# Turning keys, values and mLSTM outputs by VectorE squares and transfers instead of TensorE transposes, in a two-layer recurrent decoder step

## The chip, the cores and the metric

The kernel runs on one core of a Trainium2 chip. The metric is the device time of one execution in microseconds (us), the median over runs. The engines are named as in the profile: PE (TensorE matmuls), PEld (TensorE weight loads), DVE (VectorE), ACT (ScalarE), POOL (GpSimd), SP (the queue that issues the transfers).

## What is computed

One step of a two-layer decoder with 1024 prompt tokens and 8 sample rows that share the weights. Everything is float32. Each layer normalizes its input, projects it with one large matrix, mixes it over time in recurrent heads, multiplies by a gate and projects back:

```python
def _even_mixer(h, ...):            # layer 0
    proj = h @ w_in
    u_a, beta_pre, a_pre, q_b, k_b, v_b, if_pre, o_pre, z = _split(proj, EVEN_SPLIT)
    q_a, k_a, v_a = _split(silu(causal_conv(u_a)), ...)      # 8 gated-delta heads, key 128, value 128
    o_a, new_gdn = _gated_delta(q_a, k_a, v_a, beta, g_a, s_gdn)
    h_b, new_mc, new_mn, new_mm = _mlstm(q_b, k_b, v_b, ...)  # 8 mLSTM heads, key 64, value 128
    h_b = sigmoid(o_pre) * _rms(h_b, mlstm_norm_w)
    y = concat([_rms(o_a), h_b]) * silu(z)
    return y @ w_out, ...
def _odd_mixer(h, ...):             # layer 1
    ...                             # 4 gated linear attention heads, 4 retention heads, key 128, value 256
```

The recurrences are computed in chunks. For the gated delta rule a chunk solves a unit lower triangular system `(A + 1) U = rhs`, with `A` built from the products of keys.

## The kernel before

**Layout.** Activations lie with channels on the 128 partitions and the 1024 + 8 tokens (`W` = 1032) along the free dimension. Chunks have `L` = 128 tokens, so there are `NC` = 8 chunks. A projection of 128 output channels is 72 matmuls: three token blocks of 344, eight slices of the inner dimension, and three products, because each float32 factor is split into a high and a low part in the fast type fp32r (`halves` makes `whi` on ACT and `wlo` on DVE).

**Where a turn is needed.** The chunk recurrences need keys and values with tokens on the partitions. Before, the even layer turns them on PE: `transpose4` runs four 128x128 transposes into a PSUM bank, and DVE or ACT carries the result off while scaling it. `gdn_mix` does so for `k2` and `v2` of each of the 8 gated-delta heads (16 transposes a head, into the slots `kd` and `vs`), `mlstm_pair_mix` for the keys `mk` of each of 4 pairs of heads (8 transposes, into `kwe`), `mlstm_mix` for the values (into `va`), and `mlstm_out` turns the output `hn` of each mLSTM head back (8 transposes). In the odd layer `v_tokens` turns values with `by_token`, which is 16 DVE transposes of 32x256 for one [128, 1024] tile.

**The triangular inverse.** `inverse` takes the diagonal blocks of the 128x128 matrices `N`: it inverts 8x8 blocks on DVE (blocks fetched through DRAM by `nd` and `yd`, then seven steps of two small DVE operations), doubles them to 16 and to 32 in two passes on PE (each pass two groups of 32 products of 32x32), and then to 64 and 128.

**Order.** The program is recorded first, and every instruction gets a rank. A planner (`Recorder.order`) runs a list scheduler over the recorded operations forward and backward, with a table of assumed durations (`_cost`, `_pe_cost`, the latencies of transfers), and writes out each engine's instructions in the order that it found. The engines then run their rows strictly in that order, and a row waits for its semaphores. All transfers go through SP's one queue. The order thus interleaves the projections of coming heads with the recurrences of earlier ones. `self.nc.after` adds a dependency to all operations recorded while it is set.

**Layer boundary.** `out_proj` of the even layer loads the rows of the mixed output `y` back from DRAM (`yd`) into staging slots, splits them (`split`, ACT for the high part, DVE or POOL for the low part, into the slots `s_h` and others) and multiplies. Rows 0 to 7 are the gated-delta heads, rows 8 to 15 the mLSTM heads; the last, row 15, comes straight from `mlstm_out` of head 7. `odd_setup` loads the odd layer's constants (`lmask`, `rdm`, `rin`, `rend`, `cosT`, `sinT`), some of them into the `arena` that the even layer's small tiles used.

All instructions are issued by the recorder's helper, so all have one line in the profile (L451 before); groups are told apart by the names of their tiles.

Of the kernel before, what the change touches and what calls it, by code (L numbers as in the profile page):

```python
# [17 lines left out]
T = 1024  # L18
# [21 lines left out]
def host_constants():  # L40
# [24 lines left out]
    code = np.zeros((32, 32), f)  # L65
    for i in range(2):
        code[lm[:, 1 - i, :].T > 0] = 1.0 + i
    c["icode"] = np.tile(code, (4, 1))
    c["i8"] = np.tile(np.eye(8, dtype=f).reshape(1, 64), (128, 1))
# [39 lines left out]
def _cost(queue, method, out, args, kw):  # L109
# [4 lines left out]
    if queue == "vector":  # L114
# [4 lines left out]
        if method == "transpose":  # L119
            return 436.0, False  # L120
# [18 lines left out]
def _pe_cost(method, out, args, kw):  # L139
# [6 lines left out]
    if kw.get("tile_position") is not None and cols <= 32:  # L146
        return (max(1.87 * n / 4, 15.0) if rows > 32 else 15.0), (rows, cols)
# [319 lines left out]
class Step:  # L467
# [733 lines left out]
    def gdn_mix(self, h, k2, q2, v2, z2):  # L1201
# [4 lines left out]
        kd = self.slot("kd", [128, NC, L], name="kd")  # L1206
        ksq = self.slot("N", [128, NC, L], name="ksq")
        for g in range(2):
            p = self.transpose4(k2, g)
            p3 = p.rearrange("p (c d) -> p c d", d=L)  # L1210
            self.act(ksq[:, 4 * g:4 * g + 4, :], p3, AF.Square)
            V.tensor_tensor(kd[:, 4 * g:4 * g + 4, :], p3,
                            self.g_kdec[:, 4 * g:4 * g + 4, h].unsqueeze(2).to_broadcast([128, 4, L]), op=ALU.mult)
# [7 lines left out]
        vs = self.slot("vs", [128, NC, L], name="vs")  # L1221
        for g in range(2):
            p = self.transpose4(v2, g)
            V.tensor_tensor(vs[:, 4 * g:4 * g + 4, :], p.rearrange("p (c d) -> p c d", d=L),
                            kk[:, 2, 4 * g:4 * g + 4].unsqueeze(2).to_broadcast([128, 4, L]), op=ALU.mult)
# [31 lines left out]
        for g in range(2):  # L1257
            po = self.ps(i=g)
            for i in range(4):
# [4 lines left out]
                w = vs[:, c, :]  # L1264
                if S is not None:
                    self.mm(pc[:, 0, :], k2[:, s], S)
                    w = self.small([128, L], "w", bufs=1)
                    V.scalar_tensor_tensor(w, pc[:, 0, :], self.g_ngam[:, c, h:h + 1], vs[:, c, :], op0=ALU.mult,
# [5 lines left out]
                self.mm(pc[:, 2, :], kd[:, c, :], U)  # L1274
# [18 lines left out]
    def inverse(self, N):  # L1293
# [6 lines left out]
        by8 = lambda x: x[:, 0:256].rearrange("m (r t) -> m r t", t=32)[:, :, 0:8]  # L1300
        blocks = [slice(32 * j, 32 * j + 32) for j in range(4)]
        for j, b in enumerate(blocks):
            dma(by32(nd, j), N[b, :, b])
        n8, y8, t8 = (self.const([128, 8, 8], x) for x in ("n8", "y8", "t8"))
        dma(n8, by8(nd))
        G.tensor_copy(y8, self.i8)
        for s in range(7):
            n = 7 - s
            V.tensor_tensor(t8[:, 0:s + 1, 0:n], y8[:, 0:s + 1, s:s + 1].to_broadcast([128, s + 1, n]),
                            n8[:, s:s + 1, s + 1:8].to_broadcast([128, s + 1, n]), op=ALU.mult)  # L1310
            V.tensor_tensor(y8[:, 0:s + 1, s + 1:8], y8[:, 0:s + 1, s + 1:8], t8[:, 0:s + 1, 0:n], op=ALU.subtract)
        dma(by8(yd), y8)

        t = self.slot("EM", name="inv")
        D, At, qt, Dt = (t[:, 256 * i:256 * i + 256].rearrange("p (c t) -> p c t", c=NC) for i in range(4))
# [3 lines left out]
        for i in range(1, 3):  # L1319
            p = self.ps(None, [128, NC, 32])  # L1320
            for c in range(NC):
                for j, b in enumerate(blocks):
                    self.mm(p[b, c, :], N[b, c, b], Dt[b, c, :], tile_position=(32 * j, 32 * j))
# [623 lines left out]
    def out_proj(self, src, l, mod):  # L1947
# [107 lines left out]
        for k in late:  # L2055
            split(k)
# [197 lines left out]
```

## Time and profile before

| | |
|---|---|
| runs | 2294.88, 2287.2, 2292.83 us, median 2292.83 |
| profiled execution | 2289.05 us, span in the profile 2287.0 us |
| PE busy | 2221.4 us, 97% of the span |
| PEld busy | 2070.0 us |
| DVE busy | 1382.8 us (60%) |
| ACT, POOL busy | 747.7 us, 527.7 us |
| mean granted PE clock | 0.987 |
| transfers | 235.20 MB, mean 103 GB/s |

"Busy" is the time in which at least one instruction of an engine runs, as a share of the span. The duration of one matmul in the profile covers its way through the array, and the next starts before it ends; the pace is read from the distance of the starts. Because PE is busy nearly all the time, the idle time of other engines costs nothing unless PE waits for them.

### The profile page before, as it was taken

The page shows a single profiled execution, that of the slowest core. Times are in us where ns is not written, and L with a number is a line of the kernel's source. Part 1 is how long each engine was busy: PE and PEld are TensorE (multiplying, and loading weights), DVE is VectorE, ACT ScalarE, POOL GpSimd, SP SyncE. Part 2 cuts the span into 40 slices and gives each one's busy share as a digit, 9 for nine tenths or more (in the row PEclk, how much of TensorE's full clock was granted, in tenths as well). Part 3 has the DMA queues.
Part 4 walks back from the last instruction along what each step waited for, and adds up shares of the span by engine and source line. Part 5 has one row for each costly group of instructions (what it writes and reads, how often), then busy time and mean ns, then how long its engine had stood idle before and what let it go on. Part 6 is the DMA issues. An engine that isn't in the chain of part 4 may idle for free.

```text
span 2287.0 us, 44726 instructions
## 1 busy us (share of the span) xinstructions
PE 2221.4 (97%) x18844; PEld 2070.0 (91%) x18844; DVE 1382.8 (60%) x2700; ACT 747.7 (33%) x1374; POOL 527.7 (23%) x385
## 2 busy tenths in 40 slices
PE   6999999999999999999989999999999999998998
PEld 5777788899999999899989999999999999997997
DVE  6774646565564646556453355876976876977332
ACT  4422323232233233232331134234225324334322
POOL 3121112111123012211330031422422422433100
PEclk8999999999999999999999999999999999998999
DMA  9362544422143212432362221233142143246222
GB/s 260 124 165 60 152 133 121 129 77 72 40 118 105 69 52 86 108 95 72 114 216 84 75 76 38 56 122 107 43 136 94 50 133 95 56 149 209 74 58 91
DMA packets 285455, 235.20 MB, mean 103 GB/s; under 512 B 47819, under 2 KB 257733, under 8 KB 285246
## 3 DMA queue, kind: packets, MB, share of 16 engines
q1 hardware_dynamic: 285254, 232.35, 34.6%
q8 instruction: 147, 2.41, 0.4%
q14 instruction: 54, 0.44, 0.1%
HBM read 185.59 MB, written 46.91 MB: 102 GB/s over the span
## 4 chain that ended last, share of the span: by engine, by line
PE 88%; DMA 4%; DVE 4%; issue 1%; ACT 1%; POOL 1%; SPq 1%; POOLq 0%; DVEq 0%; ACTq 0%
PE pj L451 68%; PE A L451 14%; PE B L451 6%; DMA wf<-in_ev_w_in 1%; SPq L451 1%; DMA s_aT<-rd 0%; DVE s_h L451 0%; DMA s_h<-in_x_prompt 0%; DVE arena L451 0%; DVE s_N L451 0%; DMA s_pt<-yd 0%; DVE s_pt L451 0%; DMA ed<-s_Y 0%; DMA s_mp<-gd 0%; DVE s_mp L451 0%
## 5 line engine op out<-in xcount | busy, mean ns | idle before, releaser
L451 PE MATMUL pj<-s_h,whi 128*128 128x344 f32 (+1 forms) x6024 | 1498.6, 327 | 10.8 <-ACT s_h L451 5.4
L451 PEld LDWEIGHTS pj<-s_h,whi 128*128 128x128 f32 (+1 forms) x6024 | 1042.7, 189 | 44.8 <-issue 25.3
L451 PE MATMUL pj<-s_h,wlo 128*128 128x344 f32 (+1 forms) x3024 | 982.2, 325 | 1.5 <-DVE wlo L451 0.9
L451 PEld LDWEIGHTS pj<-s_h,wlo 128*128 128x128 f32 (+1 forms) x3024 | 569.8, 189 | 16.1 <-issue 10.6
L451 DVE TENSOR_TENSOR wlo<-wf,whi 128x1024 fp32r<-128x1024 f32 (+1 forms) x144 | 192.9, 1340 | 291.2 <-ACT whi L451 272.3
L451 ACT ACTIVATE whi<-wf 128x1024 fp32r<-128x1024 f32 (+2 forms) x146 | 152.1, 1043 | 374.9 <-PE pj L451 330.3
L451 ACT ACTIVATE s_pt<-pj 128x344 f32<-128x344 f32 (+1 forms) x170 | 77.0, 453 | 288.3 <-PE pj L451 282.8
L451 POOL TENSOR_TENSOR arena<-arena,base 128x8 f32<-128x8 f32 (+5 forms) x38 | 64.4, 1697 | 377.8 <-DVE arena L451 377.1
L451 POOL TENSOR_TENSOR s_tmp<-s_EM 128x512 f32<-128x512 f32 (+1 forms) x60 | 88.5, 1493 | 156.2 <-PE A L451 69.1
L451 DVE SCALAR_TENSOR_TENSOR s_pt<-s_u,base,s_pt 128x1024 f32<-128x1024 f32 x72 | 96.5, 1341 | 0.3
L451 ACT ACTIVATE s_u<-pj 128x344 f32<-128x344 f32 x93 | 41.9, 453 | 142.4 <-PE pj L451 80.2
L451 DVE SCALAR_TENSOR_TENSOR arena<-arena,A 128x128 f32<-128x128 f32 (+1 forms) x84 | 32.8, 391 | 84.5 <-PE A L451 83.9
L451 DVE STREAM_TRANSPOSE s_kd<-s_u 32x256 f32<-32x256 f32 x128 | 55.8, 436 | 16.6 <-ACT s_u L451 13.5
L451 POOL TENSOR_TENSOR s_tmp<-s_tmp,arena 128x1024 f32<-128x1024 f32 (+2 forms) x26 | 43.4, 1676 | 88.6 <-PE A L451 62.2
L451 POOL TENSOR_TENSOR s_kd<-s_kd,s_vs 128x1032 f32<-128x1032 f32 x8 | 21.5, 2688 | 167.6 <-ACT s_vs L451 152.2
L451 DVE SCALAR_TENSOR_TENSOR s_zz<-s_pt,pj 128x344 f32<-128x344 f32 x96 | 48.4, 507 | 18.7 <-ACT s_pt L451 17.9
L451 DVE STREAM_TRANSPOSE s_vs<-s_v 32x256 f32<-32x256 f32 x128 | 55.8, 436 | 1.9
L451 ACT ACTIVATE arena<-A,arena 128x128 f32<-128x128 f32 x64 | 23.5, 368 | 100.8 <-PE A L451 100.5
L451 ACT ACTIVATE s_tmp<-s_tmp 128x1024 f32<-128x1024 f32 (+1 forms) x44 | 46.1, 1054 | 28.7 <-POOL s_tmp L451 24.0
L451 DVE SCALAR_TENSOR_TENSOR arena<-arena,B 64x130 f32<-64x130 f32 (+1 forms) x84 | 31.2, 371 | 38.6 <-PE B L451 37.2
L451 ACT ACT_TABLE_LOAD x41 | 52.6, 1283 | 5.2 <-DMA s_h<-in_x_prompt 4.5
L451 POOL MEMSET s_u<- 128x3 f32 x24 | 2.4, 101 | 208.5 <-DVE s_pt L451 208.5
(643 smaller groups left out, 3597.7 us busy)
## 6 DMA issues: line engine op xcount, KB each, us to landing
wf<-in_ev_w_in SPq DMA_DIRECT2D x64, 512.0 KB
wf<-in_od_w_in SPq DMA_DIRECT2D x48, 512.0 KB
wf<-in_ada_w SPq DMA_DIRECT2D x32, 512.0 KB
s_pt<-yd SPq DMA_DIRECT2D x24, 516.0 KB
s_tmp<-sd SPq DMA_DIRECT2D x24, 512.0 KB
yd<-s_qg SPq DMA_DIRECT2D x15, 516.0 KB
wf<-in_ev_w_out SPq DMA_DIRECT2D x14, 512.0 KB
wf<-in_od_w_out SPq DMA_DIRECT2D x14, 512.0 KB
```

Source lines behind the costliest of these rows:

```text
L451: op.fn(*[self.placed(x) for x in op.args], **{k: self.placed(x) for k, x in op.kw.items()})
```

## The change

A new method `squares` turns a [128, 1024] tile without PE. One DVE instruction transposes all squares of 32x32 within their place and writes each with a step of 8 elements; a transfer of 512 KB puts the tile in a DRAM scratch (`td`, four of them), and four transfers of 128 KB read it back, one for each band of 32 partitions, so that the squares land in their turned place. The chunk number is then the fastest index: the slice of one chunk, `[:, c]`, has a step of 8 elements, 32 bytes, between its columns.

`squares` replaces the PE transposes of `k2` and `v2` (`gdn_mix`), `mk` (`mlstm_pair_mix`) and `hn` (`mlstm_out`); the mLSTM values stay on PE. The scaling by chunk that rode on the copy out of PSUM is now a separate DVE multiplication in place. In the odd layer `v_tokens` uses `squares` too, instead of 32 small DVE transposes a head; the turned keys there stay with `by_token`.

Other parts: `inverse` starts with 16x16 blocks on DVE (15 steps of two operations on 64 partitions) and so has one PE pass instead of two; in the odd layer every second `wlo` is made on POOL; the odd layer's constants wait for the last split of the even layer (`split_at`); the planner's assumed durations of DVE transposes and small matmuls are altered.

```diff
@@ planner @@
         if method == "transpose":
-            return 436.0, False
+            return 100 + 1.31 * n, False
...
     if kw.get("tile_position") is not None and cols <= 32:
-        return (max(1.87 * n / 4, 15.0) if rows > 32 else 15.0), (rows, cols)
+        return (max(0.8 * n, 20.0) if rows > 32 else 18.0), (rows, cols)
@@ halves @@
-        self.nc.vector.tensor_tensor(lo, w[:, 0:n], hi, op=ALU.subtract)
+        (self.nc.gpsimd if self.layer == "odd" and self.turn("half", 2) else self.nc.vector).tensor_tensor(lo, w[:, 0:n], hi, op=ALU.subtract)
@@ gdn_mix @@
-        kd = self.slot("kd", [128, NC, L], name="kd")
+        kd = self.squares(self.slot("kd", name="kd"), k2)
         ksq = self.slot("N", [128, NC, L], name="ksq")
-        for g in range(2):
-            p = self.transpose4(k2, g)
-            p3 = p.rearrange("p (c d) -> p c d", d=L)
-            self.act(ksq[:, 4 * g:4 * g + 4, :], p3, AF.Square)
-            V.tensor_tensor(kd[:, 4 * g:4 * g + 4, :], p3, ...)
+        self.act(ksq, kd, AF.Square)
+        by_c = lambda y, t: V.tensor_tensor(y, y, t.unsqueeze(1).to_broadcast([128, y.shape[1], NC]), op=ALU.mult)
+        by_c(kd.rearrange("p c d -> p d c"), self.g_kdec[:, :, h])
...
-        vs = self.slot("vs", [128, NC, L], name="vs")
-        for g in range(2):
-            p = self.transpose4(v2, g)
-            V.tensor_tensor(vs[:, 4 * g:4 * g + 4, :], ...)
+        vs = self.squares(self.slot("vs", name="vs"), v2)
+        by_c(vs.rearrange("p c d -> p d c"), kk[:, 2, :])
...
-                self.mm(pc[:, 2, :], kd[:, c, :], U)
+                self.mm(pc[:, 2, :], kd[:, c], U)
@@ inverse @@
-        for s in range(7):
+        for s in range(15):
...
-        for i in range(1, 3):
-            p = self.ps(None, [128, NC, 32])
...
+        p = self.ps(None, [128, NC, 32])
...
@@ mlstm_pair_mix @@
+        kwe = self.squares(self.slot("kwe", name="kwe"), self.mk)
+        for x in range(2):
+            t = kwe.rearrange("p c d -> p d c")[:, 64 * x:64 * x + 64, :]
+            V.tensor_tensor(t, t, self.g_we[:, :, 2 * p + x].unsqueeze(1).to_broadcast([128, 64, NC]), op=ALU.mult)
@@ mlstm_out @@
-        for g in range(2):
-            t = self.ps()
-            for i in range(4):
-                self.tr(t[:, 128 * i:128 * i + 128], hn[:, 4 * g + i, :])
-            s = slice(512 * g, 512 * g + 512)
-            V.scalar_tensor_tensor(y[:, s], t, self.nw[:, 1:2], oz[:, s], op0=ALU.mult, op1=ALU.mult)
+        t = self.squares(self.slot("va", name="ht"), hn.rearrange("p c d -> p (c d)"))
+        y3 = y[:, 0:T].rearrange("p (c t) -> p c t", c=NC)
+        V.scalar_tensor_tensor(y3, t, self.nw[:, 1:2], y3, op0=ALU.mult, op1=ALU.mult)
@@ odd_setup @@
+        self.nc.after = (self.split_at,)
         self.lmask = self.c_load("lmask", [128, 6, 32])
...
@@ new, and v_tokens @@
+    def squares(self, y, x):
+        dma = self.nc.sync.dma_start
+        y = y[:, 0:T]
+        self.nc.vector.transpose(y.rearrange("p (b j c) -> p b c j", b=4, c=NC),
+                                 x[:, 0:T].rearrange("p (c b i) -> p b c i", b=4, c=NC))
+        d = self.td[self.turn("td", 4)]
+        dma(d, y)
+        for b in range(4):
+            dma(y[32 * b:32 * b + 32].rearrange("i (a x) -> i a x", a=4),
+                d.rearrange("(a i) (b x) -> b i a x", a=4, b=4)[b])
+        return y.rearrange("p (d c) -> p c d", c=NC)
     def v_tokens(self, v):
-            self.by_token(t, v[i])
+        return [self.squares(self.slot(tag, name="vt"), v[i]) for i, tag in enumerate(("kd", "vs"))]
```

The change gives the planner other work and other durations, so all engines' rows stand in another order. Three places matter below.

PE, at the sixth gated-delta head. Before, the keys (`s_k`) are transposed between two projection matmuls (`pj`):

```order
L451 MATMUL pj_111<-s_h_604,whi_107 128x344
L451 MATMUL A_114<-base,s_k_63 128x128 x4
L451 MATMUL A_115<-base,s_k_63 128x128 x4
L451 MATMUL pj_111<-s_h_618,whi_107 128x344
L451 MATMUL pj_111<-s_h_604,wlo_109 128x344
```

After, no transposes stand there; the products of the keys with themselves (`A<-s_k`) and with the queries (`A<-s_q,s_k`) follow the projection directly:

```order
L448 MATMUL pj_111<-s_h_707,whi_107 128x344
L448 MATMUL pj_111<-s_h_727,whi_107 128x344
L448 MATMUL pj_111<-s_h_707,wlo_109 128x344
L448 MATMUL A_114<-s_k_63 128x128
L448 MATMUL A_115<-s_k_63 128x128
L448 MATMUL A_113<-s_k_63 128x128
L448 MATMUL pj_112<-s_h_447,whi_106 128x344
L448 MATMUL pj_112<-s_h_458,whi_106 128x344
L448 MATMUL pj_112<-s_h_447,wlo_108 128x344
L448 MATMUL A_114<-s_q_64,s_k_63 128x128
```

What moved: the two rows of transposes are gone from PE, and nothing of the turn is left there.

SP, the same head's key turn after the change (`td` is the scratch in DRAM, `s_kd` the turned tile):

```order
L448 DMA td_129<-s_kd_66 128x1024
L448 DMA out_s_conv<-arena 8x128
L448 DMA wf_105<-in_ev_w_in 128x8x128
L448 DMA s_kd_66<-td_129 32x4x256 x4
L448 DMA td_130<-s_vs_67 128x1024
```

What moved: five new transfers stand in the queue, the four that read back behind the one that writes, with one small transfer and one weight load between them, and the values' turn behind them.

SP, at the layer boundary. Before, constants of the odd layer (`in_rin`, `in_lmask`) stand ahead of loads of rows of `y` (`s_pt<-yd`, `s_u<-yd`):

```order
L451 DMA out_p_mc<-arena 64x128
L451 DMA out_p_mn<-arena 64x1
L451 DMA arena<-in_rin 128x512
L451 DMA arena<-in_lmask 128x192
L451 DMA s_pt_83<-yd 128x1032
L451 DMA s_pt_84<-yd 128x1032
L451 DMA s_u_79<-yd 128x1032
```

After, the same stretch holds no constants, and the last mLSTM output goes to its scratch (`td<-s_va`) behind the row loads:

```order
L448 DMA out_p_mc<-arena 64x128
L448 DMA out_p_mn<-arena 64x1
L448 DMA s_pt_83<-yd 128x1032
L448 DMA s_pt_84<-yd 128x1032
L448 DMA s_u_79<-xd 128x1032
L448 DMA s_pt_82<-yd 128x1032
L448 DMA s_pt_83<-xd 128x1032
L448 DMA wf_105<-in_ev_w_out 128x2x128 x2
L448 DMA td_132<-s_va_75 128x1024
```

What moved: the constants have gone behind the last split, and the rows of `y` follow the mLSTM outputs directly.

More of the change, by code (lines that the diff above doesn't have):

```diff
@@ L63, in host_constants @@
     c["lmask"] = np.tile(lm, (4, 1, 1)).reshape(128, 192).copy()
[L65 to L69, printed above, removed]
+    c["imask"] = np.tile(lm[:, 0, :].T, (4, 1)).copy()
+    c["i16"] = np.tile(np.eye(16, dtype=f).reshape(1, 256), (64, 1))
     sel = np.zeros((2, 4, 8, 4, 32), f)
@@ L1318, in inverse @@
         V.transpose(Dt, D)
[L1319 to L1331 removed]
+        p = self.ps(None, [128, NC, 32])
+        for c in range(NC):
+            for j, b in enumerate(blocks):
+                self.mm(p[b, c, :], N[b, c, b], Dt[b, c, :], tile_position=(32 * j, 32 * j))
+        V.tensor_tensor(At, p, self.imask.unsqueeze(1).to_broadcast([128, NC, 32]), op=ALU.mult)
+        p = self.ps(None, [128, NC, 32])
+        for c in range(NC):
+            for j, b in enumerate(blocks):
+                self.mm(p[b, c, :], At[b, c, :], D[b, c, :], tile_position=(32 * j, 32 * j))
+        V.tensor_tensor(D, D, p, op=ALU.subtract)
+        V.transpose(Dt, D)
         Y = self.slot("Y", [128, NC, L], name="Y")
@@ L1439, in mlstm_pair_mix @@
         nc, V = self.nc, self.nc.vector
-        kwe = self.slot("kwe", [128, NC, 2, 64], name="kwe")
-        for g in range(2):
-            t = self.transpose4(self.mk, g).rearrange("p (c x d) -> p c x d", c=4, x=2)
-            for x in range(2):
-                V.tensor_tensor(kwe[:, 4 * g:4 * g + 4, x, :], t[:, :, x, :],
-                                self.g_we[:, 4 * g:4 * g + 4, 2 * p + x].unsqueeze(2).to_broadcast([128, 4, 64]),
-                                op=ALU.mult)
+        kwe = self.squares(self.slot("kwe", name="kwe"), self.mk)
+        for x in range(2):
+            t = kwe.rearrange("p c d -> p d c")[:, 64 * x:64 * x + 64, :]
+            V.tensor_tensor(t, t, self.g_we[:, :, 2 * p + x].unsqueeze(1).to_broadcast([128, 64, NC]), op=ALU.mult)
         self.kwe = kwe
@@ L1672, in odd_setup @@
         nc.sync.dma_start(self.sinT, a["sinT"])
+        self.nc.after = ()
         self.glr = self.slot("va", name="glr")
@@ L2146, in build @@
             self.rd = [dr.tile([4, QB], F32, name=f"rd{i}") for i in range(2)]
-            self.nyd = {x: [dr.tile([128, 264], F32, name=f"{x}{i}") for i in range(2)] for x in ("nd", "yd")}
+            self.td = [dr.tile([128, T], F32, name=f"td{i}") for i in range(4)]
+            self.nyd = {x: [dr.tile([64, 528], F32, name=f"{x}{i}") for i in range(2)] for x in ("nd", "yd")}
             self.program()
```

56 lines of the change are left out of this document (18 added, 38 removed).

## The prediction

> **What bounds the kernel now.** I read the page first: its span, and each engine's busy time.
>
> ```profile
> span 2287.0 us, 44726 instructions
> PE 2221.4 (97%) x18844; PEld 2070.0 (91%) x18844; DVE 1382.8 (60%) x2700; ACT 747.7 (33%) x1374; POOL 527.7 (23%) x385
> ```
>
> PE sits idle for 2287.0 - 2221.4 = 65.6 us in all. Whether it is the bound everywhere is told by the view of busy time in stretches, cut at the layer boundaries (columns: stretch, its length, busy of PE, PEld, DVE, ACT and POOL with their instructions, PE's granted clock, DMA share, GB/s).
>
> ```profile
> 0.00:228.70 228.70, 197.95 (x1664) 163.66 (x1665) 145.86 (x323) 81.28 (x174) 56.66 (x72) 0.94 0.55 152
> 228.70:1143.50 914.80, 910.82 (x8339) 837.64 (x8339) 522.63 (x1194) 280.13 (x559) 183.39 (x142) 1.00 0.34 96
> 1143.50:1200.70 57.20, 49.91 (x307) 47.93 (x306) 31.11 (x41) 20.40 (x40) 18.48 (x8) 0.91 0.66 216
> 1200.70:2058.30 857.60, 853.00 (x7187) 819.22 (x7185) 582.89 (x962) 289.06 (x464) 238.05 (x149) 1.00 0.29 87
> 2058.30:2287.00 228.70, 209.68 (x1354) 201.56 (x1352) 100.32 (x182) 76.87 (x137) 31.16 (x15) 0.96 0.33 108
> ```
>
> In the even layer's steady stretch (second row) PE idles 4.0 us of 914.8, in the odd layer's (fourth row) 4.6 of 857.6. So work taken off PE in the second row is worth its full time, as long as nothing new makes PE wait; DVE's work in the fourth is worth nothing. The rest of the idle time is the start (30.8 us), the boundary between the layers (7.3) and the end (19.0). The granted clock is 1.00 in both steady stretches: there is no slow clock to win back.
>
> **The PE transposes.** They number 8 x 16 (keys and values of the gated-delta heads), 4 x 8 (mLSTM keys) and 8 x 8 (mLSTM outputs), 224. The timeline of PE shows eight of them between projection matmuls (columns: start and duration in us, then engine, operation and count).
>
> ```profile
> 773.13 0.32 PE L451 MATMUL pj<-s_h,whi 128*128 128x344 f32 x1
> 773.29 1.04 PE L451 MATMUL A<-base,s_k 128*128 128x128 f32 x8
> 774.08 0.40 PE L451 MATMUL pj<-s_h,whi 128*128 128x344 f32 x1
> 774.32 0.32 PE L451 MATMUL pj<-s_h,wlo 128*128 128x344 f32 x1
> ```
>
> From the first transpose to the next projection matmul pass 774.08 - 773.29 = 0.79 us, 0.099 us each. 224 x 0.099 = 22.2 us. The matmul behind them takes 0.24 us to the next start instead of some 0.16 (773.13 to 773.29), 0.08 us for the change of kind.
> [...]
>
> **The inverse's second pass.** One pass is two groups of 32 small products, each recorded as 64 instructions.
>
> ```profile
> 814.13 0.48 PE L451 MATMUL pj<-s_h,whi 128*128 128x344 f32 x2
> 814.54 0.75 PE L451 MATMUL A<-s_EM,s_N 32*32 32x32 f32 x64
> 815.22 0.43 PE L451 MATMUL pj<-s_h,wlo 128*128 128x344 f32 x1
> 815.49 0.48 PE L451 MATMUL pj<-s_h,whi 128*128 128x344 f32 x2
> ```
>
> A group takes 815.22 - 814.54 = 0.68 us, so 2 x 8 heads x 0.68 = 10.9 us go. Around a group 0.10 us pass before it (0.41 from 814.13 for two matmuls of 0.157) and 0.11 after. I do not take these changes of kind for every group that goes: counted in the orders, PE changes between projection, full-size and small matmuls 1196 times before and 1194 after, with 30 fewer at small groups and 26 more at full-size ones. That is 30 x 0.10 less and 13 x 0.08 more (only the change back costs there), -2 us.
>
> **The strided operand, which no row of before shows.** Turned tiles are read by PE in steps of 32 bytes. Concerned are the groups below, by form: 128 + 128 passes with `kd` and `kwe` as weights; in the odd layer four groups of 64 with turned values as weights (the third row and its like) and four of 64 in which they are streamed (the fourth and its like); with the first chunk's 16 that is 784.
>
> ```profile
> L451 PE MATMUL A<-arena,s_kd 128*128 128x128 f32 x128 | 29.8, 314 | 0.9 <-ACT arena L451 0.9
> L451 PE MATMUL B<-s_va,s_kwe 128*128 128x130 f32 x128 | 26.0, 284 | 0.1
> L451 PE MATMUL A<-s_aT,s_kd 128*128 128x128 f32 x64 | 12.7, 280 | 0.1
> L451 PE MATMUL A<-s_kd,s_N 128*128 128x128 f32 x64 | 12.5, 277 | 0.0
> 829.10 0.39 PE L451 MATMUL B<-arena,s_qs 128*128 128x130 f32 x2
> 829.33 0.39 PE L451 MATMUL B<-s_va,s_mp 128*128 128x130 f32 x2
> L451 PE MATMUL A<-s_tmp 128*32 128x32 f32 x1408 | 18.0, 199 | 0.0
> L451 DVE TENSOR_TENSOR arena<-arena 128x7 f32<-128x7 f32 x32 | 5.4, 167 | 5.5 <-DMA arena<-nd 4.9
> L451 DVE TENSOR_TENSOR arena<-arena 128x15 f32<-128x15 f32 x32 | 5.6, 174 | 0.7
> ```
>
> A pass goes at 0.115 us (829.33 - 829.10 for two). Its weights have room: 18.0 us / 1408 is 12.8 ns for 32 columns of weights, so 128 columns load in 51 ns, less than half of a pass. Nearest to the access itself is DVE's inverse: half of the 128x7 operations run over 7 rows in steps of 8 elements, and they take 167 ns against 174 for 15 elements, as their size says. I take 0. The bounds: nothing below (a step reads no faster than a row), and above it every pass doubled, 784 x 0.115 = +90 us.
>
> **The turns' latency.** A turn takes one DVE transpose, a write and four reads. Of single transfers the chain of work shows a large and a small one.
>
> ```profile
> 1155.99 2.66 DMA out_p_mn<-arena
> 1164.31 5.66 DMA s_pt<-yd
> ```
>
> A write and the reads behind it thus cost between 2 x 2.66 = 5.3 us (small) and 2 x 5.66 = 11.3 us, and I take 11 with a DVE transpose, for they move 512 KB each way. Whether that is hidden is told by the view of the tile A's instructions on PE from 700 to 900 us (minimum, median and maximum duration in ns, first and last start).
>
> ```profile
> L451 PE MATMUL A<-arena,s_kd x30: 275/275/377, 700.7 to 849.4; 128*128 128x128 f32 x30
> L451 PE MATMUL A<-base,s_k x16: 270/273/273, 773.3 to 899.1; 128*128 128x128 f32 x16
> ```
>
> One head's keys are turned from 773.3, its last chunk is done at 849.4, the next head's keys are turned from 898.3 (16 in two heads, to 899.1): of some 125 us a head its recurrence takes 76, and 11 us more still end before the next. In the new order the keys' turn stands ahead of the values' convolution, so a projection runs in between. For the turns' latency I take 3 us over the layer, in the nature of the 4.0 us that PE loses there now; a stall of 1.7 us in each of 20 places (8 gated-delta heads, 4 pairs, 8 heads of the odd layer) would eat the gain.
> If that cover is gone, behind the waiting read stand the next weight load and the row that stores an output; PE would then wait for `wlo`.
>
> **The other engines.** Prices, from rows by form:
>
> ```profile
> L451 DVE STREAM_TRANSPOSE s_EM<-s_EM 128x256 f32<-128x256 f32 x24 | 10.6, 442 | 7.1 <-DMA s_EM<-yd 6.6
> L451 DVE TENSOR_TENSOR s_kd<-A,arena 128x512 f32<-128x512 f32 x16 | 10.5, 685 | 4.7 <-ACT s_N L451 3.3 <-PE A L451 1.4
> L451 DVE TENSOR_TENSOR s_qg<-s_q,s_qg 128x1024 f32<-128x1024 f32 x8 | 9.8, 1220 | 0.1
> L451 DVE STREAM_TRANSPOSE s_vs<-s_v 32x256 f32<-32x256 f32 x128 | 55.8, 436 | 1.9
> L451 DVE TENSOR_TENSOR wlo<-wf,whi 128x1024 fp32r<-128x1024 f32 x140 | 187.0, 1336 | 282.7 <-ACT whi L451 263.7 <-PE pj L451 12.1 <-ACT s_qg L451 4.7
> 1160.24 2.51 POOL L451 TENSOR_TENSOR s_h<-s_pt,s_h 128x1032 fp32r<-128x1032 f32 x1 [0.93 <-ACT s_h L451]
> ```
>
> A transpose of 128x1024 is between 0.44 us (as 256 elements) and 1.77 (four times that); I take 1.5. In the even layer each head gains about 3.5 transposes (5.3 us), 2.5 multiplications of 1.2, 16 small operations of some 0.2, and loses four copies of 0.69 and the second pass: some +7 us, 56 in all on a DVE that is busy 522.6 of 914.8 us. In the odd layer 256 transposes of 0.436 (112 us) give way to 16, and half of 64 `wlo` go to POOL, at 2.5 us each 80 us on a POOL busy 238 of 857.6; a weight load serves 72 matmuls, 11 us. All this lies beside PE: 0. The 44 turns put 220 more transfers into SP's queue, at some 0.4 us of issue (0.85 for two in the row below), and 46 MB on the DMA engines, whose share is 0.34 and 0.29 in the steady stretches: 0.
>
> **The boundary.** There SP waited for two outputs to land before it could load odd constants over them, and the loads of `y` stood behind.
>
> ```profile
> SPq L451 <- DMA out_p_mc<-arena: 3.7, 1, 3.7
> SPq L451 <- DMA out_p_mn<-arena: 2.3, 1, 2.3
> 1163.83 0.85 SPq L451 DMA_DIRECT2D s_pt<-yd  x2
> 1177.73 1.23 PE L451 MATMUL pj<-s_h,whi 128*128 128x344 f32 x3 [5.42 <-ACT s_h L451]
> ```
>
> The constants now come later, and the loads may go up to 6 us earlier, bounded by their staging slots, of which POOL reads one until 1162.75 (1160.24 + 2.51 above). Against that the last mLSTM output takes 11 us more. Row 15 is needed last, behind 14 rows of sums for two column blocks, 252 matmuls of 0.157 or 40 us. I take -3 us, with -7 to +11 as ends.
>
> **Sum.** -22.2 - 10.9 - 2 + 0 + 3 - 3 = -35 us. The profiled execution took 2289.05 us (span 2287.0), 3.8 below the median of 2292.83. So 2254 on its scale, and 2257 on that of the medians, -1.6%. What a measurement can tell from no change is about 0.3%, 7 us.
>
> **Rivals.** First, the strided operand costs: decided from 35 / 784 = 45 ns a pass. If only the 272 streamed passes double, 272 x 0.115 = 31 us nearly cancel the gain: 2289. If weights double too, +90 gives 2347, slower. For it speaks that a third of a pass is enough; against it the slack of the weight loads and the DVE row.
> [...]
> Second, the turns come late: stalls of 1 us in 20 places take 20 us, 2277; of 2 us, 2297. For it: one SP queue, where reads wait for a landing. Against: DVE waits only 6.6 us in all for the inverse's transfers, which run through DRAM too (the transpose row above). Third, the boundary loses 11 us for the last output: 2271, still faster. Fourth, the gain is not there, because PE's time is not the limit; the steady rows speak against it.
>
> **Chances.** The forecast, 2243 to 2268 with the boundary's ends and the runs' scatter: 0.66. Late turns or a bad boundary that leave part (2268 to 2286): 0.14. Nothing measurable (2286 to 2300), by streamed operands alone or stalls of 1.7 to 2 us: 0.08. Slower, by both strided operands or longer stalls: 0.12. So faster 0.80, same 0.08, slower 0.12. The range for 8 in 10 goes from 2241 into the second case, to 2285; only the slower cases lie far beyond.
>
> **What will show it.** The even layer's stretch shortens by some 33 us with PE still idle under 1% of it; the odd layer's stays at 857, with DVE busy 130 us less there. The passes with `s_kd` and `s_kwe` keep 0.115 us between starts. If the strided rival is right, these starts spread, and the odd layer's stretch grows by 31 us or more. If the turns are late, PE's waits name DVE's `arena`, `s_N` or `wlo`, and DVE's own waits name transfers from `td`. Behind the boundary PE waits under 5 us.

## The result, and the profile after

The changed kernel takes 2366.8 us (median of 4 runs, 2364.03 to 2368.59) against 2290.86 for the kernel before: a ratio of 1.033, interval 1.0307 to 1.0353. The prediction was 2257, range 2241 to 2285. It is slower by 76 us where 34 us less were forecast.

The page of the kernel after, its first lines (span, busy time and instructions of each engine):

```profile
span 2362.1 us, 42524 instructions
PE 2287.1 (97%) x17596; PEld 2128.9 (90%) x17596; DVE 1344.6 (57%) x2527; ACT 756.9 (32%) x1366; POOL 604.4 (26%) x409
```

PE issues 1248 instructions less than before and is busy 65.7 us longer; its idle time is 75.0 us instead of 65.6. So most of the loss is not waiting: something that PE still does has become dearer. The groups by form (busy us, mean ns) name it. These four answer to four groups that the prediction showed at 29.8, 26.0, 12.7 and 12.5 us:

```profile
L448 PE MATMUL A<-arena,s_kd 128*128 128x128 f32 x128 | 44.9, 433 | 0.0
L448 PE MATMUL B<-s_va,s_kwe 128*128 128x130 f32 x128 | 41.9, 410 | 4.5 <-DVE s_kwe L448 2.9 <-DVE arena L448 0.7 <-issue 0.7
L448 PE MATMUL A<-s_aT,s_kd 128*128 128x128 f32 x64 | 20.0, 395 | 0.0
L448 PE MATMUL A<-s_kd,s_N 128*128 128x128 f32 x64 | 20.1, 404 | 0.0
```

The same work on the same shapes, but read with a step of 32 bytes: 15.1 and 15.9 us more for the two weight groups of the even layer, and 62.7 more for the odd layer's eight groups, which go from 12.3 to 12.7 us each to 20.0 to 20.6. Together 93.7 us in 768 passes, 0.122 us a pass. (The other 16 of the prediction's 784 passes are those of the first chunk.) The weight loads tell the two kinds apart (PEld groups of the kernel after, busy us and mean ns; before, the first two took 188 and 192 ns, the third 190):

```profile
L448 PEld LDWEIGHTS A<-arena,s_kd 128*128 128x128 f32 x128 | 35.5, 325 | 7.8 <-ACT arena L448 6.5
L448 PEld LDWEIGHTS A<-s_aT,s_vs 128*128 128x128 f32 x64 | 17.8, 326 | 0.0
L448 PEld LDWEIGHTS A<-s_kd,s_N 128*128 128x128 f32 x64 | 10.2, 197 | 0.2
```

Where the turned tile is the weights, the load itself grows by some 136 ns; where it is streamed (third row), the load stays almost as it was (197 ns after 190) and the matmul grows instead (404 ns after 277). Both cost about the same: in the odd layer's 256 passes of each kind 31.1 us as weights and 31.6 streamed, 0.121 and 0.123 us a pass.

To split the rest by place I cut the span at the first matmul of the odd layer's low-rank projection (`pj<-s_h,s_N`). In the kernel after, and in all versions of it below that have no PE transposes and keep its changes to the odd layer, 10109 PE instructions stand ahead of it, so the cut means the same work. In the other kernels up to 22 instructions of the odd layer stand on the other side of it, some 3 us at 0.157 us each. Busy time in the two stretches, before and then after (length; busy of PE, PEld, DVE, ACT, POOL; clock; DMA share; GB/s):

```profile
0.00:1369.70 1369.70, 1326.21 (x11365) 1216.15 (x11366) 766.67 (x1687) 417.65 (x833) 276.46 (x242) 0.99 0.38 109
1369.70:2287.00 917.30, 895.14 (x7481) 853.88 (x7479) 616.13 (x1013) 330.08 (x541) 251.26 (x143) 0.99 0.31 94
```

```profile
0.00:1393.10 1393.10, 1329.83 (x10109) 1218.03 (x10110) 847.80 (x1778) 423.08 (x823) 284.04 (x235) 0.98 0.47 129
1393.10:2362.10 969.00, 957.26 (x7489) 910.83 (x7488) 496.79 (x750) 333.82 (x543) 320.37 (x176) 0.99 0.36 106
```

The odd part is 51.7 us longer: 62.7 of dearer passes less some 10 us of idle time. The even part is 23.4 us longer although 1248 PE instructions have gone (8 more have moved behind the cut) and the dearer passes add only 31: PE idles 63.3 us there instead of 43.5, at a lower mean clock and a fuller DMA. Of PE's longest waits from 100 to 1240 us (total us, times, longest), these name tiles of the heads' recurrences, and the last the boundary:

```profile
PE A L448 <- DVE s_tmp L448: 7.2, 4, 3.9
PE A L448 <- DVE s_N L448: 5.3, 3, 3.7
PE A L448 <- DVE s_EM L448: 3.4, 2, 2.9
PE B L448 <- DVE s_kwe L448: 2.9, 2, 2.1
PE A L448 <- DVE s_q L448: 2.8, 1, 2.8
PE pj L448 <- ACT s_h L448: 2.1, 1, 2.1
```

Before, over the whole span, PE's longest wait for such a tile is `s_mp`'s; `s_EM` is far smaller, and the boundary's is larger:

```profile
PE B L451 <- DVE s_mp L451: 5.5, 3, 4.4
PE A L451 <- DVE s_EM L451: 1.0, 2, 0.9
PE pj L451 <- ACT s_h L451: 5.4, 1, 5.4
```

Two suspects follow: the step, and something in the even layer that the removal of PE work does not pay for. The experiments take them one by one. Each median below was taken beside runs of the kernel before with a median of 2286 to 2289 us. The kernel after was timed only beside the 2290.86 above, so differences from it are a few us less certain than the ratios.

### The profile page after: what moved, and what is told of

Same layout as the page of the kernel before. It is cut to its first block, busy times and chain, and to the rows that moved or that the text cites. A ratio compares the mean times of both kernels' runs of the same rounds, so it can differ in the third digit from the quotient of the medians.

```text
span 2362.1 us, 42524 instructions
## 1 busy us (share of the span) xinstructions
PE 2287.1 (97%) x17596; PEld 2128.9 (90%) x17596; DVE 1344.6 (57%) x2527; ACT 756.9 (32%) x1366; POOL 604.4 (26%) x409
## 4 chain that ended last, share of the span: by engine, by line
PE 58%; DVE 4%; DMA 3%; issue 1%; ACT 1%; SPq 0%; POOL 0%; POOLq 0%; DVEq 0%; ACTq 0%
PE pj L448 43%; PE A L448 10%; PE B L448 5%; DMA s_pt<-yd 1%; DVE arena L448 1%; SPq L448 0%; DVE s_pt L448 0%; DVE s_zz L448 0%; DMA s_kd<-td 0%; DVE wlo L448 0%; DVE s_va L448 0%; DVE s_h L448 0%; DVE s_N L448 0%; DMA s_vs<-td 0%; DMA sd<-s_tmp 0%
## 5 line engine op out<-in xcount | busy, mean ns | idle before, releaser
L448 DVE TENSOR_TENSOR wlo<-wf,whi 128x1024 fp32r<-128x1024 f32 x112 | 148.1, 1323 | 234.0 <-ACT whi L448 210.2
L448 ACT ACTIVATE whi<-wf 128x1024 fp32r<-128x1024 f32 (+1 forms) x146 | 152.2, 1042 | 398.1 <-PE pj L448 324.0
L448 POOL TENSOR_TENSOR wlo<-wf,whi 128x1024 fp32r<-128x1024 f32 (+1 forms) x32 | 78.4, 2450 | 154.0 <-ACT whi L448 153.6
L448 DVE TENSOR_TENSOR s_EM<-s_EM 64x15 f32<-64x15 f32 (+7 forms) x240 | 47.1, 196 | 15.1 <-DMA s_EM<-nd 9.6
L448 POOL TENSOR_TENSOR s_aT<-s_aT,s_q 128x1032 f32<-128x1032 f32 x8 | 24.8, 3099 | 120.3 <-ACT s_aT L448 120.3
```

The source lines that it names most:

```text
L448: op.fn(*[self.placed(x) for x in op.args], **{k: self.placed(x) for k, x in op.kw.items()})
```

## Experiments on the step

**A step, and nothing else.** The kernel before, with the turned tiles stored chunk-fastest (DVE writes them so), `by_chunk` being a view:

```diff
-        kd = self.slot("kd", [128, NC, L], name="kd")
+        kd = self.by_chunk(self.slot("kd", name="kd"), 8)   # "p (g d s) -> p g s d", s=8
...                                                          # kwe and the odd layer's vt alike
```

> The kernel before, with the keys, the mLSTM keys and the odd layer's values stored chunk-fastest (a step of 8 elements, 32 bytes, between the columns that TensorE reads) and nothing else changed; TensorE's rows stand in almost the same order. Theory A, the step costs some 0.12 us on each of the 784 passes whether as weights or streamed: +94 us over before, about 2385 us, and the groups with s_kd, s_kwe and s_vs show 400 ns and more a pass as they do after the change. Theory B, the loss after the change comes from late turns and the new order, and the longer passes there are only a sign of waiting: within 7 us of before.

Measured: 2399.67 us, ratio 1.0475 (1.0441 to 1.0508), +110 us. Its page:

```profile
span 2399.2 us, 44722 instructions
PE 2316.7 (97%) x18844; PEld 2163.5 (90%) x18844; DVE 1431.5 (60%) x2700; ACT 747.2 (31%) x1374; POOL 519.9 (22%) x385
```

PE is busy 95.3 us longer than before with the same 18844 instructions; that is theory A's 94. The other 16.9 us of the span are idle time of PE, which is why the total stands above the 2385 expected. DVE is 48.7 us busier, since its writes with a step are dearer too (a 32x256 transpose takes 669 to 680 ns instead of 436), and PE waits 11.7 us for DVE's `s_mp` (5.5 before). Theory B falls: the step costs this without any turn through DRAM.

**Smaller steps.** The same with 2 elements for `s_kd` and 4 for `s_kwe` and `s_vs`:

```diff
-        kd = self.by_chunk(self.slot("kd", name="kd"), 8)
+        kd = self.by_chunk(self.slot("kd", name="kd"), 2)
-        kwe = self.by_chunk(self.slot("kwe", name="kwe"), 8)
+        kwe = self.by_chunk(self.slot("kwe", name="kwe"), 4)
...                                                          # odd layer: first tile 2, second 4
```

> As the run with a step of 8, but with smaller steps: 2 elements (8 bytes) for the gated-delta keys s_kd and for the odd layer's first value tile (s_kd there), 4 elements (16 bytes) for the mLSTM keys s_kwe and the second value tile (s_vs). Theory A1, what counts is whether two columns fall into the same 16 bytes: the groups with step 2 keep 280 to 314 ns, those with step 4 cost what step 8 costs (64 + 64 passes of kwe, 256 of s_vs, 16 of the first chunk: 384 + 8 passes x 0.12 = +47 us, 2338). Theory A2, the cost grows with the distance: step 2 costs a quarter and step 4 half of step 8, 0.03 and 0.06 us a pass, +35 us, 2326. Theory A3, any step costs all of it: +94, 2385. Theory B: no change.

Measured: 2333.61 us, ratio 1.0193 (1.0163 to 1.0224), +44 us, nearest to theory A1's 47. The groups decide (step 2 first, then step 4; the last two rows are the transposes with which DVE writes them, 436 ns before):

```profile
L451 PE MATMUL A<-arena,s_kd 128*128 128x128 f32 x128 | 29.9, 315 | 0.9 <-ACT arena L451 0.9
L451 PE MATMUL A<-s_kd,s_N 128*128 128x128 f32 x64 | 12.5, 276 | 0.0
L451 PE MATMUL B<-s_va,s_kwe 128*128 128x130 f32 x128 | 40.7, 398 | 1.9 <-issue 1.8
L451 PE MATMUL A<-s_aT,s_vs 128*128 128x128 f32 x64 | 19.5, 387 | 0.0
L451 PE MATMUL A<-s_vs,s_N 128*128 128x128 f32 x64 | 19.7, 398 | 0.0
L451 DVE STREAM_TRANSPOSE s_kd<-s_u 32x256 f32<-32x256 f32 x128 | 55.9, 437 | 17.1 <-ACT s_u L451 13.9 <-PE A L451 0.9
L451 DVE STREAM_TRANSPOSE s_vs<-s_v 32x256 f32<-32x256 f32 x128 | 80.8, 631 | 1.8
```

A step of 8 bytes costs next to nothing (29.9 against 29.8 us, 12.5 against 12.5; all five groups with it 81.4 against 79.9 us, 0.004 us a pass), a step of 16 bytes costs nearly what 32 bytes cost: 0.115 us a pass for `s_kwe` (40.7 - 26.0 over 128) and for `s_vs` streamed (19.7 - 12.3 over 64). Theories A2 and A3 fall. DVE's writes have their edge at the same place: 437 ns at 8 bytes, 631 at 16, and 669 to 680 at 32 in the run before this one. So the price stands at 16 bytes and not at 8; no step between the two was run, so theory A1's numbers are borne out, and the reason it gives for them is not shown.

**The odd layer without the step.** The kernel after, the odd layer's values turned by `by_token` as before:

```diff
-        return [self.squares(self.slot(tag, name="vt"), v[i]) for i, tag in enumerate(("kd", "vs"))]
+        ...                                                 # as before: self.by_token(t, v[i])
```

> The changed kernel with the odd layer's values turned as before (32x256 DVE transposes, side by side); the even layer keeps the turns through DRAM and the step. Theory A: 528 passes of the 784 lose their step, some 63 us less than after, 2304; up to the low-rank projection of the odd layer nothing changes (1393 us). If the side-by-side tiles gave only 54 us because a faster TensorE waits more everywhere, the odd part gives clearly less than 63 here; if that happens only in the even layer, all of it comes.

Measured: 2309.2 us (2299.93 to 2314.78), 58 less than after. By the cut, the even part is 1396.0 us (after 1393.1) and the odd part 917.0 (after 969.0, before 917.3). The odd layer gives back the 52 us by which it had become longer, a little less than its 63 us of passes, since some waiting returns with them (PE idles 18.4 us there, 11.7 after).

**Side by side for TensorE.** The kernel after, the turned tile landing in a `tmp` slot; the scaling that follows anyway writes it side by side into `s_kd` or `s_kwe`, and in the odd layer ACT copies it. The even layer's `vs` keeps the step: PE reads it in 16 passes only (the first chunks), DVE in every other chunk.

```diff
-        kd = self.squares(self.slot("kd", name="kd"), k2)
+        kr = self.squares(self.slot("tmp", name="kr"), k2)
+        kd = self.slot("kd", [128, NC, L], name="kd")
...
-        by_c(kd.rearrange("p c d -> p d c"), self.g_kdec[:, :, h])
+        V.tensor_tensor(kd, kr, self.g_kdec[:, :, h].unsqueeze(2).to_broadcast([128, NC, L]), op=ALU.mult)
```

> The changed kernel, but TensorE reads no step: the turned tiles land in a tmp slot, the scaling of the keys writes them side by side into s_kd and s_kwe (no instruction more), and in the odd layer an ACT copy writes the values side by side (16 copies of about 1.1 us more on ACT). Theory A: 94 us less than after, about 2273 us; what then stays above 2256 (before less the 35 us of removed work) is what the turns and the new order cost. Theory B (the turns' waits cost it all): within 10 us of after, 2357 to 2377.

Measured: 2312.8 us, ratio to before 1.0105 (1.007 to 1.014). All eight odd groups are back at 12.4 to 12.6 us, `s_kd` is at 30.2 and `s_kwe` at 28.3, and PE's busy time falls by 79.5 us to 2207.6; but the time falls by 54, not the 94 of theory A. PE now idles 105.7 us. So the step was not all: this kernel is still 23 us slower than before, where the removed work had promised 35 us less. Two things of the experiment's own remain in it. The step has moved to the engines that read the turned tile: ACT's squares of the keys take 2204 ns, and 1055 where the source lies side by side (the run of the detour below), the odd layer's copies 2.3 us where 1.1 were expected, and DVE's sums with `vs` are as dear as in the kernel after, 462 ns (first here, then with turns on DVE alone, where `vs` has no step):

```profile
L448 DVE SCALAR_TENSOR_TENSOR arena<-A,arena,s_vs 128x128 f32<-128x128 f32 x56 | 25.8, 461 | 28.4 <-PE A L448 28.4
L448 DVE SCALAR_TENSOR_TENSOR arena<-A,arena,s_vs 128x128 f32<-128x128 f32 x56 | 19.6, 350 | 28.1 <-PE A L448 28.0
```

And the tile passes through one slot more.

## Experiments on what is left

**The inverse alone.** The kernel before with the 16x16 blocks of `inverse` and nothing else:

```diff
-        for s in range(7):
+        for s in range(15):
...
-        for i in range(1, 3):
-            p = self.ps(None, [128, NC, 32])
+        p = self.ps(None, [128, NC, 32])
```

> The kernel before with the inverse alone changed: 16x16 blocks on DVE in 15 steps of two operations, one PE pass instead of two; no turns, the planner's durations as before. Prediction's term: 10.9 us less and up to 1 us of mode changes, 2279 us. Rival: the longer DVE chain (30 small operations of about 0.2 us instead of 14, 3 us more a head) is on the path that PE waits for in the even layer, and the gain is lost: 2288 to 2295.

Measured: 2272.35 us, ratio 0.9922 (0.9896 to 0.9948), -17 us: the rival falls, this part wins, and by more than the 11 to 12 us expected. Only 7.6 us of it lie ahead of the cut (1362.1 against 1369.7); the other 9.7 lie in the odd layer (907.6 against 917.3; some 2 us of this is the cut's own shift, 13 instructions), where no inverse is computed. What came there the mechanism does not explain.

**The even layer without turns through DRAM.** The kernel after with the even layer's turns back on PE; the odd layer's values turned by transfers and copied side by side:

```diff
-        kd = self.squares(self.slot("kd", name="kd"), k2)
+        ...                                                 # kd, vs, kwe and hn as before: self.transpose4
```

> The changed kernel with the even layer's turns back on TensorE as before, and the odd layer's values turned by transfers and copied side by side by ACT; the 16x16 inverse, the later constants, POOL's half of wlo and the planner's durations as after. Theory that the even layer's turns are where the 57 us go: near the run with the inverse alone, 2272, or a few us better by the boundary (2262 to 2275). If the odd layer's turns, the planner's new durations or the moved constants lose it: 2285 or more.

Measured: 2289.75 us, ratio 1.0005 (0.9994 to 1.0015), outside what the theory gave and inside the other case's 2285 or more. By the cut, the even part takes 1363.2 us, as in the run with the inverse alone (1362.1); the odd part is 922.6 against 907.6. So the even layer loses nothing without its turns, as the theory says, and the total misses because of the odd part. That part has the detour through `tmp` and ACT, which costs about that much (see the run of the detour below).

**Turns without transfers.** The kernel after, with every turn made by DVE straight into its place:

```diff
     def squares(self, y, x):
-        ...                                                 # one transpose, one write, four reads
+        y = y[:, 0:T].rearrange("p (c d) -> p c d", c=NC)
+        self.by_token(y, x)                                 # 16 transposes of 32x256
+        return y
```

> The changed kernel with every turn made by 16 DVE transposes of 32x256 that put the squares straight into their place (as the odd layer did before): no transfers, no step, the same order of the program; some 7.0 us of DVE for a turn instead of 2.2, 28 turns in the even layer or +134 us on DVE there. With side-by-side tiles the changed kernel took 2313 us where the removed work allows 2256, so 57 us are lost to something else. Theory T, the turns' way through DRAM (landing times of 5 to 8 us and the fuller transfer engines) makes TensorE wait: without it 2250 to 2270. Theory D, DVE's added work in the even layer makes it wait: no better than 2313, rather 2320 to 2340. Theory P, the planner's wrong durations: in between, since 32x256 transposes are planned at their true 0.436 us.

Measured: 2267.58 us, ratio 0.9911 (0.9883 to 0.994). The same PE work as side by side, 45 us faster, with a DVE that is busy 1560.6 us instead of 1368.4. Theory D falls. The even parts, side by side and then with these turns:

```profile
0.00:1383.10 1383.10, 1307.19 (x10109) 1193.46 (x10110) 862.56 (x1778) 423.23 (x823) 286.00 (x235) 0.97 0.47 129
```

```profile
0.00:1342.70 1342.70, 1291.29 (x10109) 1180.99 (x10110) 966.05 (x2198) 415.08 (x823) 279.54 (x234) 0.98 0.40 112
```

40.4 us in the same 10109 PE instructions: 24.5 are idle time, the other 15.9 are PE busy longer at a lower mean clock (0.97 against 0.98). Against the added idle time stand two waits for weights, 15.8 us, which are the longest of PE in the run side by side (60 to 1340 us):

```profile
PE pj L448 <- ACT whi L448: 15.8, 2, 9.0
```

The second of them, 6.72 us up to 393.24, fits what the prediction named as a danger: SP issues the weight load at 385.75, right behind the four reads of a turned tile (`s_va<-td`, from 383.65 to 385.58). At the first, 9.04 us up to 134.11, the last read of a turned tile was issued 15 us ahead of the weight load, so that wait is not shown to be the turns'.

**The transfers as a load.** The run before, plus the turns' transfers, whose data nobody uses (a write to the scratch, and four copies from there to another scratch):

```diff
         self.by_token(y, x)
+        dma(d, y.rearrange("p c d -> p (c d)"))
+        for b in range(4):
+            dma(e[32 * b:32 * b + 32].rearrange("i (a x) -> i a x", a=4),
+                d.rearrange("(a i) (b x) -> b i a x", a=4, b=4)[b])
```

> The run with turns by 32x256 DVE transposes (2268 us), with the transfers of the changed kernel's turns added as a load that nobody waits for: each turned tile is also written to the scratch (512 KB), and four transfers of 128 KB copy the scratch to another scratch. Theory T2, it is the load on the transfer engines and on SP's queue that makes weight loads and the inverse's blocks late: most of the 45 us between that run and the one with side-by-side tiles comes back, 2290 to 2315. Theory T1, it is the turn's own latency, the head that waits for its own tile: 2262 to 2275.

Measured: 2286.75 us, ratio to before 0.9994 (0.9977 to 1.0011): 19 of the 45 us come back, 3 us short of theory T2's range and 12 above T1's. In the even part it is clearer:

```profile
0.00:1373.50 1373.50, 1298.95 (x10109) 1185.21 (x10109) 967.60 (x2198) 413.75 (x823) 277.92 (x234) 0.98 0.46 130
```

1373.5 us: 30.8 of the 40.4 us return though no head waits for a turned tile. (Both are single executions; the one with turns on DVE alone lay 4 us under the median of its runs.) PE's idle time in this part grows from 51.4 to 74.6 us. The wait that grows most is for `s_EM`, from 60 to 1340 us, first with turns on DVE alone, then with the load, where it is PE's longest:

```profile
PE A L448 <- DVE s_EM L448: 1.6, 2, 1.3
```

```profile
PE A L448 <- DVE s_EM L448: 14.3, 6, 7.2
```

`s_EM` holds the inverse's blocks, which go through DRAM as well. DVE's own wait for them doubles (total, times, longest; without and with the load):

```profile
DVE s_EM L448 <- DMA s_EM<-yd: 14.4, 4, 11.2
```

```profile
DVE s_EM L448 <- DMA s_EM<-yd: 29.3, 7, 10.3
```

Two heads, the fourth and the sixth, hold 12.75 of PE's 14.3 us. The timelines of the fourth, without and with the load, show where the blocks become late:

```profile
564.21 1.81 SPq L448 DMA_DIRECT2D s_EM<-yd  x4
568.85 0.45 DVE L448 STREAM_TRANSPOSE s_EM<-s_EM 128x256 f32<-128x256 f32 x1 [0.21 <-DMA s_EM<-yd]
```

```profile
578.96 1.82 SPq L448 DMA_DIRECT2D s_EM<-yd  x4
590.18 0.45 DVE L448 STREAM_TRANSPOSE s_EM<-s_EM 128x256 f32<-128x256 f32 x1 [5.89 <-DMA s_EM<-yd]
```

From the last of the four issues to DVE's start pass 2.8 us without the load and 9.4 with it (1.5 and 9.6 in the sixth head). So in these two heads the small reads are late behind their issue, and not because SP issued them late. The copies of a turned tile had been issued 9 and 12 us ahead of them, with a few other transfers between, so that the copies hold them up is likely but not seen. The odd layer, which has turns through DRAM too but no inverse, loses nothing to the load (912.3 us against 918.6). So the turns' transfers cost the even layer mostly as traffic, 31 of 40 us; that they do it through the inverse's small reads is seen for the 12.7 us in so far as the reads are late, and argued for the rest. The other 10 us were not separated: the turned tile's own lateness, the steps that DVE and ACT still read side by side, and the new order are all in them.

**The planner's durations.** Side by side, the planner told 2.2 us for a large transpose (it assumed 1.44) and 2.5 us more for each transfer to or from `td`:

```diff
-            return 100 + 1.31 * n, False
+            return (2200.0 if n == 1024 else 100 + 1.31 * n), False
...
+        op.more = 2500.0 if queue == "sync" and any(x.name.startswith("td") for x in writes + reads) else 0.0
```

> The run with side-by-side tiles (2313 us) with the planner alone told better durations: 2.2 us for a 128x1024 DVE transpose (it assumed 1.44) and 2.5 us more for every transfer to or from the turns' scratch. Theory P, the 57 us are an order made on wrong durations: 2256 to 2275. Theory T, the transfers themselves delay others whatever the order: 2300 or more.

Measured: 2297.07 us, ratio to before 1.0043 (1.0028 to 1.0058), between the theories. The even part falls from 1383.1 to 1361.5 us, about half of the 40. An order made with longer durations thus avoids part of the loss, not all.

**The mLSTM outputs alone.** The inverse, and `hn` turned by transfers, which PE never reads:

```diff
-            self.tr(t[:, 128 * i:128 * i + 128], hn[:, 4 * g + i, :])
...
+        t = self.squares(self.slot("va", name="ht"), hn.rearrange("p c d -> p (c d)"))
```

> The kernel before with the 16x16 inverse and with the mLSTM outputs alone turned by transfers (8 turns, never read by TensorE; planner's durations as before). Prediction's terms: 64 transposes x 0.099 = 6.3 us below the run with the inverse alone (2272), 2266, if the boundary loses nothing. Theory T: each of these turns ends at a row that is needed soon, 1 to 2 us each and up to 11 at the boundary: 2275 to 2290.

Measured: 2279.58 us, ratio 0.9961 (0.9947 to 0.9975): 7 us above the run with the inverse alone instead of 6 below; the even part goes from 1362.1 to 1375.0. That eight turns in the place of 64 PE transposes win 6 us is not borne out; the 13 us in the even part are about what a new order alone moves (next run).

**The order by itself.** The kernel before with the planner's two new durations:

```diff
-            return 436.0, False
+            return 100 + 1.31 * n, False
...                                                          # and the durations of the small matmuls
```

> The kernel before with the planner's two new durations alone (DVE transposes, small matmuls): the same instructions in another order. Prediction took this as 0: 2288, within 7 us. If a new order by itself can cost or win as much as single terms of the prediction: 8 us or more away from 2288, either way.

Measured: 2280.26 us (2275.34 to 2294.87), ratio 0.998 (0.9956 to 1.0003), not told from no change, and between the two cases expected. In its profiled execution, the slowest of the ten, the even part is 11.6 us longer than before and the odd part 5.5 shorter. Differences of some 10 us between kernels whose order was planned anew I therefore do not explain; that holds for single terms of this size above and below.

**The detour.** Side by side with its `tmp` slots and ACT copies, the turns on DVE:

```diff
         kr = self.squares(self.slot("tmp", name="kr"), k2)
...
     def squares(self, y, x):
+        y = y[:, 0:T].rearrange("p (c d) -> p c d", c=NC)
+        self.by_token(y, x)
```

> The run with side-by-side tiles, with its way through the tmp slots and its ACT copies in the odd layer kept, but each turn made by 32x256 DVE transposes without transfers. It tells whether that run's waits (2313 us against 2268 with direct turns) belong to the transfers or to the experiment's own detour: transfers, 2260 to 2280; detour, 2295 or more.

Measured: 2282.3 us, ratio 0.9985 (0.9972 to 0.9997): just above the range for "transfers". The even part is 1343.3 us as with direct turns (1342.7), the odd part 932.2 instead of 918.6. So the detour costs some 14 us, all in the odd layer, and none of the 40 us in the even layer. The odd part side by side with transfers is 930.2 us, so the transfers themselves cost the odd layer nothing.

**The best version.** Turns on DVE and the inverse, without the changes for the odd layer, and the same with the old durations:

```diff
-        (self.nc.gpsimd if self.layer == "odd" and self.turn("half", 2) else self.nc.vector).tensor_tensor(...)
+        self.nc.vector.tensor_tensor(lo, w[:, 0:n], hi, op=ALU.subtract)
-        self.nc.after = (self.split_at,)
```

> The run with turns by 32x256 DVE transposes, without the changes for the odd layer: all of wlo on DVE, the odd constants loaded where the kernel before loads them; the planner's new durations stay. From the places of the odd layer's low-rank projection: the even part took 1342.7 us there, the odd part 918.6 against 907.6 in the run with the inverse alone. If POOL's share of wlo or the moved constants cost those 11 us: about 2255. If not: 2262 to 2270.

```diff
-            return 100 + 1.31 * n, False
+            return 436.0, False
```

> As the run before it, and with the planner's old durations too (0.436 us for every DVE transpose, which is right for 32x256; the old ones of the small matmuls). If the new durations only reshuffle the order: within 8 us of that run. If they are needed for the gain: 2270 or more.

Measured: 2265.17 us, ratio 0.9899 (0.9876 to 0.9922), and 2273.19 with the old durations, 0.9937 (0.9915 to 0.996). The first is the fastest kernel of this study, 1% under before and 4% under after, though not told apart from the run with direct turns (0.9911). The 11 us of the odd layer were not found: its part is 913.3 us here. The second differs by 8.02 us, just outside the first case's 8 and inside the second's 2270 or more; by what a new order alone moves, it decides nothing.

## Why the prediction was wrong

The parts, in the profiled executions' time, are differences of neighbouring runs at the cut, so that they add up proves nothing; the runs above have to carry them. Removed work, with turns on DVE: -27.0 (1342.7 - 1369.7). Turns through DRAM in the even layer, with the steps that DVE and ACT read: +40.4 (1383.1 - 1342.7). The step in the even layer: +10.0 (1393.1 - 1383.1) for 31 us of passes; idle time falls from 75.9 to 63.3 us there, so some of the passes seem to lie where PE would have waited. The step in the odd layer: +52.0 (969.0 - 917.0), where transfers cost nothing. The rest of the odd layer: -0.3. Sum +75.1, which is 2362.1 - 2287.0. The terms of 10 us and less are no larger than what a new order alone moved; the others are.

- **What bounds the kernel, and the work removed: right.** PE's busy time fell by 31.3 us with turns on DVE (2221.4 to 2190.1), forecast 33.1 without the changes of kind. DVE's saving in the odd layer was worth nothing, as said: side by side it is busy 505.86 us there, in the run of the detour 593.30, and the odd parts take 930.2 and 932.2 us.
- **"I take 0" for the strided operand: the step that failed.** It measured 94 to 95 us of PE's busy time, close to the upper bound of 90 that stood beside it; 62 us of it came through to the span after the change. Both reasons for the lower end were rows of another thing. The 51 ns was scaled up from the busy time of matmuls with 32 columns of weights that lie side by side; the load of 128 columns is recorded with 188 ns, and with 325 when it has a step. The DVE row was 7 elements long and half of its operations had no step; over 256 elements a step of 32 bytes takes DVE from 436 to 680 ns. With bounds of 0 and 90 us the near row carried the whole forecast. The first rival, 2347, had the mechanism right.
- **The turns' latency, 3 us, and the load of 46 MB, 0: the second failure.** Measured 40 us in the even layer with PE's operands side by side, 31 of them with the load alone. The prediction set 46 MB against a mean share of the DMA engines of 0.34; but single small reads became late, 9.4 us behind their issue where 2.8 had passed. Its argument that DVE waits only 6.6 us in all for the inverse's transfers also misread its rows: the row of 128x7 operations that it shows has another 4.9 us, for `nd`. The second rival's price for 2 us in 20 places, 40 us, is the number that came, but by luck: it meant turned tiles that come late, and most of what came returned with nobody waiting for a turned tile. Of weight loads behind a waiting read, the danger that it named, one wait of 6.7 us fits.
- **The two rivals together.** Taken one by one they gave 2347 and 2297. Added they would give 2387. The 20 us less are a net: 62 us of the step instead of 90, and 27 us of removed work instead of the 38 forecast with the boundary.
- **The boundary:** PE waits 2.1 us for `s_h` there instead of 5.4, and under the 5 forecast. That is 3 us less, as taken; what else the moved constants did to the time was not measured apart.
- **The transposes' price:** 2.2 us each on DVE, not 1.5; what that cost PE was not measured apart.

## What to carry to other kernels

Count the distance between the elements that TensorE reads before counting what a layout saves: fp32 with a step of 8 bytes was almost free here (0.004 us a pass), with 16 and with 32 each 128x128 pass cost 0.115 and 0.122 us more on a pace of 0.115, as weights and streamed alike. A price between far bounds wants a row of the same engine with the same access; where there is none, the forecast belongs between the bounds and not at the end that the nearest row suggests. Work moved from a saturated engine to transfers can be paid for by small transfers that the engine's next work needs (here the inverse's blocks of two heads, 9.4 and 9.6 us behind their issue instead of 2.8 and 1.5), so look at these one by one, from issue to landing, and not at the mean share.

## What was unexpected in the hardware

- TensorE's operands in float32: 0.122 us more for a 128x128 pass at a step of 32 bytes, 0.115 at 16 bytes, 0.004 at 8 bytes. A weight load with a step of 32 bytes is recorded with 325 ns instead of 188.
- DVE's writes have the same edge: a 32x256 transpose takes 437 ns at 8 bytes, 631 at 16, 669 to 680 at 32.
- ACT's reads with a step of 32 bytes: a square over 128x1024 takes 2204 ns instead of 1055.
- 31 us of dearer passes added only 10 us to the even layer, where PE also waits. The two kernels' orders differ, so this is one case and not a rule.
